# Linear attention with the states of two heads as blocks on a diagonal, and the levels of both pairs ahead of the chunks

## The chip, the cores and the metric

The kernel runs on one core of a Trainium2 chip. The metric is the time of one execution in microseconds (us) on the device. A core has five engines with an instruction stream each: PE (products), DVE, ACT and POOL (elementwise work) and SP, which issues the transfers here.

## The reference

One layer of a decoder for 2048 prompt tokens and 8 x 4 sample tokens, width 1024, in fp32. A mixer runs two kinds of heads beside each other, then there is cross-attention over 256 memory tokens, then a gated MLP with a convolution. The change lies in the gated linear attention (GLA) of the mixer: 4 heads, keys of 64 and values of 128 columns, evaluated in chunks:

```
q, k, v, r, a, u, sv = split_cols(xn @ w_in)
logg = log_sigmoid(a @ w_alpha + b_alpha) / 16
# per chunk, with b the running sum of logg in it:
scores = einsum('bihd,bjhd,bijhd->bijh', q, k, exp(b_i - b_j) where j <= i)
o = scores @ v + (q * exp(b)) @ S
S = exp(b_last) * S + (k * exp(b_last - b))^T @ v
# afterwards
o = rmsnorm(o, g_gla_out) * silu(r)
s_out = gelu(u) * z          # z: causal mixing of sv in chunks of 128
y = concat([o, s_out]) @ w_out
```

## The kernel before

The prompt goes through in four blocks s = 0 to 3 of 512 tokens; the 32 sample tokens ride along with block 1 in the mixer and with block 2 in the MLP. Names carry the block first: `v20` is tile 0 of v in block 2, `op213` is pair 1, chunk 3 in block 2.

A wide fp32 product is done as three products of split operands (hi by hi, lo by hi, hi by lo; lines L92 to L94), which accumulate in one of four PSUM banks of the pool accp. The projection of a block is a row of such steps: `t_ws` (sv), `a_wk`, `a_wq`, `t_wv` (v), `a_wu` (u), `t_wr` (r); then comes the output projection `a_wo`. A result is copied from its bank by DVE (v, r; L800) or goes through gelu on ACT (u, sv), and the next step's product that takes the bank waits for that. The split of a weight takes ACT (h_...) and DVE (l_..., L85).

The GLA goes two heads (a pair p) at a time, with 64 + 64 key columns on the 128 partitions. `sel` is a mask of 128 x 2 with a column for each head. Its steps for a pair:

- `diag`: the diagonal of the scores (pr on POOL, dgp on PE, dgs on DVE, P on ACT).
- seven `level` steps: level l gives the scores between the two halves of blocks of 2^(l+1) tokens. DVE subtracts (e), ACT takes exp, DVE makes kr (two instructions, one for each head), POOL multiplies e by k, PE makes s (four products), DVE copies s into P of both heads under a mask. `s206` is level 6 of pair 0 in block 2.
- `decay`: exp(b) on ACT; qz, which is q times exp(b) times sel, one tile for each head, on DVE; ebl (exp(b) at each chunk's end); kh, and its transpose ktp, which DVE copies to kt.
- four `chunk` steps (128 tokens): op on PE (for each head P times v, then qz times S, 128 columns each), which DVE copies to o; kv on PE, for each head a product of its 64 key columns on a half of the 128 x 64 positions; then DVE updates S, of 128 x 128, into the other of two buffers.

The sample's state has a step of its own (`smp`) in block 1. The tail: `onorm` (squares of o on ACT, L825, sums in oss; then rt on DVE, L298, and ors on POOL, L299), `silu` of r on ACT, `gate` (o times ors times r, DVE L1113), `back` (transposes otp, and the split ch20 to ch23). The SGU has zp on PE, z on DVE (L865), z times u on POOL (L875), and the split into ch24 to ch27 (ACT, L84) and cl24 to cl27 (POOL, L85); a_wo takes all eight.

The order in the program comes from `weave`: the projection's steps and w_out's are the main row, and a part (steps, first, last) is spread evenly over the main steps first to last. `gla_steps` returned its steps and its tail, and the call had the numbers:

```
(gla[:2], 5, 7), (gla[2:12], 8, 10), (gla[12:], 10, 13), (gtail, 16, 18)
```

`gla[:2]` are the gates and pair 0's running sums; `gla[2:12]` diag, pair 1's sums, seven levels and decay of pair 0; the rest four chunks of pair 0, then diag, levels, decay and chunks of pair 1. A scheduler then sets the order on each engine from the dependencies and its own estimate of durations; tiles come from rotating pools (49 wide ones in `up`), and every engine runs its stream in order.

## Time and profile before

| | us |
|---|---|
| median of 3 runs | 2885.29 |
| lowest, highest run | 2882.75, 2885.83 |
| the profiled execution, its own time | 2885.16 |
| its span, first to last instruction | 2883.4 |
| PE busy | 2847.6 |
| DVE busy | 1792.6 |
| ACT busy | 1055.3 |
| POOL busy | 667.6 |

The mean granted clock of PE is 0.998. A row of the timeline gives the start in us, the length in us, the engine, the line, the operation, out<-in, the shapes and the count of instructions that were put together; in brackets the idle time of the engine before it and what ended it. A fp32 product that isn't split appears as two records. A row of the waits names who waited for whom: us in total, times, longest.

From 1588 to 1725 us, the linear attention of block 2 with the work around it, PE is busy for 134.60 of 137.00 us, DVE for 104.66, ACT for 65.71 and POOL for 39.61.

### The profile page before, as it was taken

How to read it: one execution, taken by the hardware profiler on the slowest of the kernel's cores; microseconds unless marked ns; L12 is line 12 of the kernel's file. 1: busy time of each engine (PE TensorE's matmuls, PEld its weight loads, DVE VectorE, ACT ScalarE, POOL GpSimd, SP SyncE). 2: the span in 40 equal slices, each digit the busy share in tenths (PEclk: the TensorE clock that was granted, in tenths of full speed). 3: DMA queues.
4: the chain of work that ended last, by engine and by line, in shares of the span. 5: the costliest groups of instructions: out<-in, count | busy, mean ns of one | idle time of the engine just before them, and what ended most of it. 6: DMA issues, size and time to landing. Idle time of an engine off the chain costs nothing.

```text
span 2883.4 us, 47388 instructions
## 1 busy us (share of the span) xinstructions
PE 2847.6 (99%) x18148; PEld 2517.3 (87%) x18148; DVE 1792.6 (62%) x3101; ACT 1055.3 (37%) x1908; POOL 667.6 (23%) x700
## 2 busy tenths in 40 slices
PE   8999999999999999999999999999999999999998
PEld 8888988888888798888887889899999888899998
DVE  7568468777656645555556773566666675474555
ACT  5536344334364423222124453422223534331221
POOL 1213112111132311222222221222223132132221
PEclk9999999999999999999999999999999999999999
DMA  9646579999932245878995214577775323577775
GB/s 311 198 153 210 186 251 339 328 338 335 336 103 61 67 145 184 299 277 277 322 319 192 74 45 165 197 254 258 260 268 199 107 71 107 181 257 262 278 279 182
DMA packets 359626, 625.49 MB, mean 217 GB/s; under 512 B 26683, under 2 KB 227326, under 8 KB 359400
## 3 DMA queue, kind: packets, MB, share of 16 engines
q1 hardware_dynamic: 359400, 622.46, 63.7%
q8 instruction: 144, 2.36, 0.3%
q14 instruction: 82, 0.67, 0.1%
HBM read 497.04 MB, written 125.31 MB: 216 GB/s over the span
## 4 chain that ended last, share of the span: by engine, by line
PE 92%; DVE 4%; ACT 2%; issue 1%; POOL 1%; DMA 0%; DVEq 0%; SPq 0%; POOLq 0%; ACTq 0%
PE d L92 6%; PE d L94 6%; PE d L93 6%; PE sc L94 2%; PE sc L93 2%; PE sc L92 2%; PE a_wo L92 2%; PE a_wo L94 2%; PE a_wo L93 2%; PE a_wx L92 2%; PE a_wx L94 2%; PE a_wx L93 2%; PE a_wup L93 1%; PE a_wg L93 1%; PE a_wg L92 1%; PE a_wg L94 1%
## 5 line engine op out<-in xcount | busy, mean ns | idle before, releaser
L92 PE MATMUL d<-acth,whi_wd 128*128 128x512 f32 (+2 forms) x720 | 244.9, 340 | 4.9 <-DVE h L1546 4.9
L93 PE MATMUL d<-actl,whi_wd 128*128 128x512 f32 (+2 forms) x720 | 242.7, 337 | 0.0
L94 PE MATMUL d<-acth,wlo_wd 128*128 128x512 f32 (+2 forms) x720 | 242.6, 337 | 0.0
L1546 DVE TENSOR_TENSOR h<-d,h 128x512 f32<-128x512 f32 (+1 forms) x232 | 133.0, 581 | 150.0 <-PE d L94 149.7
L1485 POOL TENSOR_TENSOR c<-c,bc_f 128x512 f32<-128x512 f32 (+1 forms) x88 | 137.6, 1567 | 140.0 <-ACT c L1484 139.3
L92 PEld LDWEIGHTS d<-acth,whi_wd 128*128 128x128 f32 x720 | 135.5, 188 | 20.4 <-DVE h L1546 5.7
L94 PEld LDWEIGHTS d<-acth,wlo_wd 128*128 128x128 f32 x720 | 135.2, 188 | 15.8 <-issue 1.6
L93 PEld LDWEIGHTS d<-actl,whi_wd 128*128 128x128 f32 x720 | 135.4, 188 | 14.4 <-issue 1.2
L1475 ACT ACTIVATE c<-g,colsb 128x512 f32<-128x512 f32 x88 | 71.7, 815 | 206.1 <-DVE g L1444 154.3
L92 PE MATMUL sc<-whi_qk,woh 128*128 128x256 f32 x512 | 144.3, 283 | 0.0
L94 PE MATMUL sc<-whi_qk,wol 128*128 128x256 f32 x512 | 144.3, 282 | 0.0
L93 PE MATMUL sc<-wlo_qk,woh 128*128 128x256 f32 x512 | 143.9, 282 | 0.0
L1507 POOL TENSOR_TENSOR c<-r_q_wup,c 128x512 f32<-128x512 f32 (+1 forms) x33 | 58.7, 1779 | 341.7 <-DVE r_q_wup L279 221.5
L1472 POOL COPY carry<-g 128x2 f32<-128x2 f32 x88 | 30.8, 350 | 435.1 <-DVE g L1444 433.0
L984 POOL TENSOR_TENSOR e<-e,k 128x512 f32<-128x512 f32 (+1 forms) x48 | 69.2, 1441 | 238.6 <-DVE kr L980 168.4
L92 PE MATMUL a_wo<-ch,h_wo 128*128 128x512 f32 (+1 forms) x320 | 113.3, 358 | 5.1 <-ACT ch L84 4.0
L94 PE MATMUL a_wo<-ch,l_wo 128*128 128x512 f32 (+1 forms) x320 | 113.2, 354 | 0.0
L93 PE MATMUL a_wo<-cl,h_wo 128*128 128x512 f32 (+1 forms) x320 | 112.9, 353 | 0.0
L1476 DVE SCALAR_TENSOR_TENSOR c<-g,colsb,c 128x512 f32<-128x512 f32 x88 | 86.0, 977 | 30.7 <-ACT c L1475 30.1
L92 PE MATMUL a_wx<-pTh,whi_wx 128*128 128x512 f32 x256 | 101.2, 395 | 0.0
L94 PE MATMUL a_wx<-pTh,wlo_wx 128*128 128x512 f32 x256 | 100.4, 392 | 0.0
L93 PE MATMUL a_wx<-pTl,whi_wx 128*128 128x512 f32 x256 | 100.3, 392 | 0.0
(3354 smaller groups left out, 9526.2 us busy)
## 6 DMA issues: line engine op xcount, KB each, us to landing
whi_wd<-wd SPq DMA_DIRECT2D x66, 512.0 KB
wlo_wd<-wd SPq DMA_DIRECT2D x66, 512.0 KB
r_wo<-in_w_out_dram SPq DMA_DIRECT2D x32, 512.0 KB
whi_qk<-qkd SPq DMA_DIRECT2D x32, 512.0 KB
wlo_qk<-qkd SPq DMA_DIRECT2D x32, 512.0 KB
wlo_wx<-vod SPq DMA_DIRECT2D x32, 512.0 KB
whi_wx<-vod SPq DMA_DIRECT2D x32, 512.0 KB
r_wg<-in_w_gate_dram SPq DMA_DIRECT2D x22, 512.0 KB
```

The costliest lines, as they stand in the source:

```text
L92: pe.matmul(ps, wh, xh, start=first, stop=False)
L93: pe.matmul(ps, wh, xl, start=False, stop=False)
L94: pe.matmul(ps, wl, xh, start=False, stop=last)
L984: pool.tensor_tensor(kl[:, :Tl], e[:, :Tl], B.k[p][:, :Tl], ALU.mult)
L1472: pool.tensor_copy(carry[:, f, :], g[:, SB:SB + 2])
L1475: act.activation(c[:, :SB], g[:, 2:SB + 2], AF.Identity, bias=cb, scale=w2)
L1476: dve.scalar_tensor_tensor(c[:, :SB], g[:, 1:SB + 1], w1, c[:, :SB], ALU.mult, ALU.add)
L1485: pool.tensor_tensor(c[:, :T], c[:, :T], B.fbc[:, :T], ALU.mult)
L1507: (dve, pool)[i].tensor_tensor(c[:, :T], q[i], c[:, :T], ALU.mult)
L1546: dve.tensor_tensor(B.h[m + mm][:, cs], ps[:, :cw], B.h[m + mm][:, cs], ALU.add)
```

## The change

- S of a pair is a tile of 128 x 256 with the two heads' states of 64 x 128 as blocks on its diagonal and zeros elsewhere. Two such tiles for each pair are set to zero at the start (POOL) and used in turn.
- qz is one tile for each pair, without sel.
- `chunk`: op is first one product of qz with S, 256 columns, and then two of P with v, 128 columns each; kv is one product of 128 x 256, of which the blocks on the diagonal are used; S is updated by two DVE instructions of 64 x 128.
- The squares of o are taken in `chunk` (and `smp`) after pair 1 of that chunk.
- `smp` masks qz for each head on DVE first (qm).
- The order: outside block 1, levels of pair 0 over main steps 7 to 9, levels of pair 1 over 9 to 12, and then all eight chunks over 12 to 14. In block 1 the parts stand as before.
- The final state leaves in four transfers in place of two; `up` has 48 wide tiles in place of 49.

```diff
-NU, NT, NRAW, NW = 49, 6, 5, 5
+NU, NT, NRAW, NW = 48, 6, 5, 5
...
-        t = cp.tile([128, 128], F32, tag=f"S{p}", name=f"Sz{p}", bufs=2)
-        pool.memset(t, 0.0)
-        state[p] = t
+        state[p] = [const([128, 256], f"S{p}{i}") for i in range(2)]
+        for t in state[p]:
+            pool.memset(t, 0.0)
...
-            for hh in range(2):
-                z = U(f"qz{s}{p}{hh}")
-                dve.scalar_tensor_tensor(z[:, :T], B.q[p][:, :T], sel[:, hh:hh + 1], e0[:, :T], ALU.mult, ALU.mult)
-                B.qz[2 * p + hh] = z
+            z = U(f"qz{s}{p}")
+            dve.tensor_tensor(z[:, :T], B.q[p][:, :T], e0[:, :T], ALU.mult)
+            B.qz[p] = z
...
-            S = state[p]
+            S, Sn = state[p]
             cs = slice(c * 128, (c + 1) * 128)
+            pe.matmul(ps[:, :256], B.qz[p][:, cs], S, start=True, stop=False)
             for hh in range(2):
                 h = 2 * p + hh
-                os_ = slice(hh * 128, (hh + 1) * 128)
-                pe.matmul(ps[:, os_], B.P[h][:, cs], B.v[c][:, h * 128:(h + 1) * 128], start=True, stop=False)
-                pe.matmul(ps[:, os_], B.qz[h][:, cs], S, start=False, stop=True)
+                pe.matmul(ps[:, hh * 128:(hh + 1) * 128], B.P[h][:, cs], B.v[c][:, h * 128:(h + 1) * 128],
+                          start=False, stop=hh == 1)
             dve.tensor_copy(B.o[c][:, p * 256:(p + 1) * 256], ps[:, :256])
             kv = mps(f"kv{s}{p}{c}")
+            pe.matmul(kv[:, :256], B.kt[p][:, cs], B.v[c][:, p * 256:(p + 1) * 256], start=True, stop=True)
             for hh in range(2):
-                h = 2 * p + hh
-                pe.matmul(kv[hh * 64:(hh + 1) * 64, :128],
-                          B.kt[p][:, c * 128 + hh * 64:c * 128 + (hh + 1) * 64],
-                          B.v[c][:, h * 128:(h + 1) * 128], start=True, stop=True)
-            Sn = cp.tile([128, 128], F32, tag=f"S{p}", name=f"S{s}{p}{c}", bufs=2)
-            dve.scalar_tensor_tensor(Sn, S, B.eb[p][:, c:c + 1], kv[:, :128], ALU.mult, ALU.add)
-            state[p] = Sn
-            if s == NSB - 1 and c == 3:
-                nc.sync.dma_start(o_state_gla[0, 0, 2 * p:2 * p + 2].rearrange("hh d v -> (hh d) v"), Sn)
+                rows, os_ = slice(hh * 64, (hh + 1) * 64), slice(hh * 128, (hh + 1) * 128)
+                dve.scalar_tensor_tensor(Sn[rows, os_], S[rows, os_], B.eb[p][rows, c:c + 1], kv[rows, os_],
+                                         ALU.mult, ALU.add)
+                if s == NSB - 1 and c == 3:
+                    nc.sync.dma_start(o_state_gla[0, 0, 2 * p + hh], Sn[rows, os_])
+            state[p] = Sn, S
+            if p == 1:
+                norm_of(B.o[c], B.oss, c, 128)
...
-                pool.tensor_tensor(qm3, blkbc, B.qz[h][:, SB:TM].unsqueeze(1).broadcast_to([128, 8, NS]), ALU.mult)
+                dve.tensor_scalar(qm[:, 256:288], B.qz[p][:, SB:TM], sel[:, hh:hh + 1], None, ALU.mult)
+                pool.tensor_tensor(qm3, blkbc, qm[:, 256:288].unsqueeze(1).broadcast_to([128, 8, NS]), ALU.mult)
...
-            for c in range(nt):
-                norm_of(B.o[c], B.oss, c, 128 if c < 4 else NS)
             rstd_of20(B.ors, B.oss, sample, 1.0 / 128)
...
+        if sample:
+            parts = [(head, 5, 7), (pairs[0], 8, 10), (ends[0] + pairs[1] + ends[1], 10, 13), (tail, 16, 18)]
+        else:
+            parts = [(head, 5, 7), (pairs[0], 7, 9), (pairs[1], 9, 12), (ends[0] + ends[1], 12, 14), (tail, 16, 18)]
```

How the order moves, at three places of block 2.

PE in the kernel before, from the first chunk of pair 1 on (S113 and S210 are the states after the chunks 113 and 210):

```order
L1052 MATMUL op210_16874<-v20_16404,P210_16536 128x128
L1053 MATMUL op210_16874<-S113_9584,qz210_16811 128x128
L1052 MATMUL op210_16874<-v20_16404,P211_16541 128x128
L1053 MATMUL op210_16874<-S113_9584,qz211_16813 128x128
L1058 MATMUL kv210_16880<-v20_16404,kt21_16826 64x128 x2
L1052 MATMUL op211_16885<-v21_16405,P210_16536 128x128
L1058 MATMUL kv211_16891<-v21_16405,kt21_16826 64x128 x2
L1052 MATMUL op212_16896<-v22_16406,P210_16536 128x128
L1053 MATMUL op211_16885<-S210_16883,qz210_16811 128x128
```

PE in the changed kernel at the same place (S10 and S11 are the two tiles for the state of pair 1):

```order
L1050 MATMUL op210_16832<-S10_245,qz21_16729 128x256
L1053 MATMUL op210_16832<-v20_16466,P210_16416 128x128
L1053 MATMUL op210_16832<-v20_16466,P211_16421 128x128
L1057 MATMUL kv210_16837<-v20_16466,kt21_16742 128x256
L1050 MATMUL op211_16845<-S11_246,qz21_16729 128x256
L1053 MATMUL op211_16845<-v21_16467,P210_16416 128x128
L1053 MATMUL op211_16845<-v21_16467,P211_16421 128x128
L1057 MATMUL kv211_16850<-v21_16467,kt21_16742 128x256
L862 MATMUL zp22_16888<-wsT_688,sv20_15897 128x128
```

The products of P with v and the next kv stood ahead of the products with S210; now op211 begins with the product with S11, which DVE makes from kv210, the row just ahead.

DVE in the kernel before, from the masks of level 3 of pair 0 on (e205 and kr205 belong to level 5, kh20 to decay):

```order
L995 COPY_PREDICATED P200_16272<-mask3_129,s203_16370 128x32x8
L995 COPY_PREDICATED P201_16277<-mask3_129,s203_16370 128x32x8
L800 COPY v20_16404<-t_wv20_16205 128x512
L980 SCALAR_TENSOR_TENSOR kr205_16434<-e205_16430,sel_153,q20_16142 128x256 x2
L969 TENSOR_TENSOR e206_16445<-b20_16197 128x4x64
L970 TENSOR_TENSOR e206_16445<-b20_16197 128x4x64
L995 COPY_PREDICATED P200_16272<-mask4_135,s204_16385 128x16x16
L995 COPY_PREDICATED P201_16277<-mask4_135,s204_16385 128x16x16
L800 COPY v21_16405<-t_wv21_16212 128x512
L800 COPY v22_16406<-t_wv22_16219 128x512
L980 SCALAR_TENSOR_TENSOR kr206_16449<-e206_16445,sel_153,q20_16142 128x256 x2
L1020 TENSOR_TENSOR kh20_16468<-b20_16197 128x512
```

DVE in the changed kernel, from the masks of level 6 of pair 0 on (e211 and e212 are levels 1 and 2 of pair 1, dgs21 its diagonal):

```order
L996 COPY_PREDICATED P200_16210<-mask6_147,s206_16383 128x4x64
L996 COPY_PREDICATED P201_16215<-mask6_147,s206_16383 128x4x64
L970 TENSOR_TENSOR e211_16439<-b21_16225 128x128x2
L971 TENSOR_TENSOR e211_16439<-b21_16225 128x128x2
L1032 COPY kt20_16405<-ktp20_16400 128x512
L85 TENSOR_TENSOR l_wr20_16457<-r_wr20_16454,h_wr20_16456 128x1024
L945 COPY dgs21_16408<-dgp21_16407 128x8
L981 SCALAR_TENSOR_TENSOR kr211_16443<-e211_16439,sel_153,q21_16137 128x256 x2
L970 TENSOR_TENSOR e212_16492<-b21_16225 128x64x4
L971 TENSOR_TENSOR e212_16492<-b21_16225 128x64x4
L800 COPY v20_16466<-t_wv20_16173 128x512
L800 COPY v21_16467<-t_wv21_16180 128x512
```

The copy of v20 stood between the masks of level 3 and kr of level 5 of pair 0; now it stands behind pair 0's last masks, kt20, the split l_wr20 and two levels' worth of pair 1.

POOL in the kernel before, the end of the SGU, and ors:

```order
L875 TENSOR_TENSOR z22_16953<-z22_16953,u22_16723 128x512
L875 TENSOR_TENSOR z23_16995<-z23_16995,u23_16750 128x512
L299 TENSOR_TENSOR ors2_17041<-rt_17058,neghalf_88 128x16
L85 TENSOR_TENSOR cl26_16957<-z22_16953,ch26_16956 128x512
L85 TENSOR_TENSOR cl27_16999<-z23_16995,ch27_16998 128x512
```

POOL in the changed kernel, the same five instructions:

```order
L875 TENSOR_TENSOR z22_16893<-z22_16893,u22_16671 128x512
L85 TENSOR_TENSOR cl26_16897<-z22_16893,ch26_16896 128x512
L299 TENSOR_TENSOR ors2_16749<-rt_17006,neghalf_88 128x16
L875 TENSOR_TENSOR z23_16961<-z23_16961,u23_16698 128x512
L85 TENSOR_TENSOR cl27_16965<-z23_16961,ch27_16964 128x512
```

z23 times u went ahead of ors and now goes behind it; cl26 went behind ors and now goes ahead. On PE the first products of a_wo took ch24 to ch26 and left cl26, ch27 and cl27 for later; now they take ch24 to ch27 with their cl in a row.

More of the change, by code (lines that the diff above doesn't have):

```diff
@@ L1045, in chunk @@
                 B.o = [U(f"o{s}{i}") for i in range(nt)]
+                B.oss, B.ors = narrow(f"oss{s}", 20), narrow(f"ors{s}", 20)
             ps = mps(f"op{s}{p}{c}")
-            S = state[p]
+            S, Sn = state[p]
             cs = slice(c * 128, (c + 1) * 128)
+            pe.matmul(ps[:, :256], B.qz[p][:, cs], S, start=True, stop=False)
             for hh in range(2):
                 h = 2 * p + hh
-                os_ = slice(hh * 128, (hh + 1) * 128)
-                pe.matmul(ps[:, os_], B.P[h][:, cs], B.v[c][:, h * 128:(h + 1) * 128], start=True, stop=False)
-                pe.matmul(ps[:, os_], B.qz[h][:, cs], S, start=False, stop=True)
+                pe.matmul(ps[:, hh * 128:(hh + 1) * 128], B.P[h][:, cs], B.v[c][:, h * 128:(h + 1) * 128],
+                          start=False, stop=hh == 1)
             dve.tensor_copy(B.o[c][:, p * 256:(p + 1) * 256], ps[:, :256])
             kv = mps(f"kv{s}{p}{c}")
+            pe.matmul(kv[:, :256], B.kt[p][:, cs], B.v[c][:, p * 256:(p + 1) * 256], start=True, stop=True)
             for hh in range(2):
-                h = 2 * p + hh
-                pe.matmul(kv[hh * 64:(hh + 1) * 64, :128],
-                          B.kt[p][:, c * 128 + hh * 64:c * 128 + (hh + 1) * 64],
-                          B.v[c][:, h * 128:(h + 1) * 128], start=True, stop=True)
-            Sn = cp.tile([128, 128], F32, tag=f"S{p}", name=f"S{s}{p}{c}", bufs=2)
-            dve.scalar_tensor_tensor(Sn, S, B.eb[p][:, c:c + 1], kv[:, :128], ALU.mult, ALU.add)
-            state[p] = Sn
-            if s == NSB - 1 and c == 3:
-                nc.sync.dma_start(o_state_gla[0, 0, 2 * p:2 * p + 2].rearrange("hh d v -> (hh d) v"), Sn)
+                rows, os_ = slice(hh * 64, (hh + 1) * 64), slice(hh * 128, (hh + 1) * 128)
[6 more added lines that the diff above has]
+                norm_of(B.o[c], B.oss, c, 128)
         sgd = state_gla[0].rearrange("b (p hh) d v -> (hh d) b p v", hh=2)
@@ L1083, in smp @@
             dve.tensor_copy(B.o[4][:NS, p * 256:(p + 1) * 256], ps[:NS, :256])
+            if p == 1:
+                norm_of(B.o[4], B.oss, 4, NS)
             for i in range(2):
@@ L1099, in onorm @@
         def onorm():
-            B.oss, B.ors = narrow(f"oss{s}", 20), narrow(f"ors{s}", 20)
-            for c in range(nt):
-                norm_of(B.o[c], B.oss, c, 128 if c < 4 else NS)
             rstd_of20(B.ors, B.oss, sample, 1.0 / 128)
@@ L1127, in back @@
             B.cat[h] = (hi, lo)
-        out = [gates, lambda: cums(0)]
+        head, pairs, ends = [gates, lambda: cums(0)], [], []
         for p in range(2):
-            out.append(lambda p=p: diag(p))
-            if p == 0:
-                out.append(lambda: cums(1))
-            out += [lambda p=p, l=l: level(p, l) for l in range(7)]
-            out.append(lambda p=p: decay(p))
-            out += [lambda p=p, c=c: chunk(p, c) for c in range(4)]
-            if sample:
-                out.append(lambda p=p: smp(p))
+            pairs.append([lambda p=p: diag(p)] + ([lambda: cums(1)] if p == 0 else [])
+                         + [lambda p=p, l=l: level(p, l) for l in range(7)] + [lambda p=p: decay(p)])
+            ends.append([lambda p=p, c=c: chunk(p, c) for c in range(4)] + ([lambda p=p: smp(p)] if sample else []))
         tail = [onorm] + [lambda c=c: silu(c) for c in range(nt)] + [lambda c=c: gate(c) for c in range(nt)]
         tail += [lambda h=h: back(h) for h in range(4)]
-        return [Step(f) for f in out], [Step(f) for f in tail]
+        if sample:
+            parts = [(head, 5, 7), (pairs[0], 8, 10), (ends[0] + pairs[1] + ends[1], 10, 13), (tail, 16, 18)]
+        else:
+            parts = [(head, 5, 7), (pairs[0], 7, 9), (pairs[1], 9, 12), (ends[0] + ends[1], 12, 14), (tail, 16, 18)]
+        return [([Step(f) for f in x], i, j) for x, i, j in parts]
     def out_proj_steps(B, unit, src, g, name, sample, first, finished, keep=None, seven=False,
@@ L1624, in hymba_step_kernel @@
         proj = proj_steps(B)
-        gla, gtail = gla_steps(B)
+        gla = gla_steps(B)
         sgu_st = sgu_steps(B)
@@ L1636, in hymba_step_kernel @@
         folds = [(qk_steps, 0, 10), (vo_steps, 11, 19)] if s == 0 else []
-        steps += weave(proj + w1, *folds, (after, 0, 5), (sgu_st[:1], 6, 6), (sgu_st[1:nst], 11, 11), (sgu_st[nst:], 12, 15), (gla[:2], 5, 7), (gla[2:12], 8, 10), (gla[12:], 10, 13), (gtail, 16, 18))
+        steps += weave(proj + w1, *folds, (after, 0, 5), (sgu_st[:1], 6, 6), (sgu_st[1:nst], 11, 11), (sgu_st[nst:], 12, 15), *gla)
         scales, sc, turns = attention_steps(B)
```

## The prediction

> **What bounds the kernel.** I read the page first (busy shares, the chain that ended last), then the waits of PE, then the timeline of PE, DVE, ACT and POOL around the linear attention. The first two rows below are the page's, the others the waits of PE.

> ```profile
> PE 2847.6 (99%) x18148; PEld 2517.3 (87%) x18148; DVE 1792.6 (62%) x3101; ACT 1055.3 (37%) x1908; POOL 667.6 (23%) x700
> ...
> PE 92%; DVE 4%; ACT 2%; issue 1%; POOL 1%; DMA 0%; DVEq 0%; SPq 0%; POOLq 0%; ACTq 0%
> ...
> PE a_wo L92 <- ACT ch L84: 4.0, 2, 2.0
> ...
> PE s L991 <- POOL e L984: 1.9, 4, 1.1
> ...
> PE op L1052 <- DVE o L1054: 0.6, 1, 0.6
> ```

> PE is busy for 99% of the span and is 92% of the chain. A change can win in two ways only: less time on PE, or fewer of the few microseconds in which PE waits. It loses when PE comes to a product whose operand is late. The profiled execution took 2885.16 us, the median of the three runs is 2885.29; the sum is made against 2885.2. A measurement of this kernel can tell about 0.2% (5.8 us) from no change.

> **The products (PE).** The timeline of PE in block 0, where products of a chunk stand among those of the projection, then a product of 256 columns (lgp, whose 8 records are 4 products):

> ```profile
> 201.53 0.39 PE L92 MATMUL a_wu<-xh,h_wu 128*128 128x512 f32 x1
> 201.76 0.40 PE L93 MATMUL a_wu<-xl,h_wu 128*128 128x512 f32 x1
> 202.09 0.44 PE L1058 MATMUL kv<-v,kt 128*64 128x128 f32 x4
> 202.46 0.49 PE L1052 MATMUL op<-v,P 128*128 128x128 f32 x2
> 202.88 0.44 PE L1058 MATMUL kv<-v,kt 128*64 128x128 f32 x4
> 203.24 0.50 PE L94 MATMUL a_wu<-xh,l_wu 128*128 128x512 f32 x1
> 203.58 0.40 PE L92 MATMUL a_wu<-xh,h_wu 128*128 128x512 f32 x1
> ...
> 127.91 1.99 PE L911 MATMUL lgp<-wal,aT 33*128 33x256 f32 x8
> ```

> A wide product starts 0.23 after the one ahead (201.53, 201.76), so without the chunk the next would start at 201.99. It starts at 203.24, and the one behind it 0.34 later instead of 0.23: the insertion cost 1.25 + 0.11 = 1.36. An op of 128 columns is 0.22 (below, 1700.93 to 1701.15), so two kv pairs cost 1.14, one 0.57, though its four records are only 0.44 long. A chunk before is 4 x 0.22 + 0.57 = 1.45. A record of 256 columns takes (1.99 - 0.39) / 7 = 0.23, a product two of them, 0.46. A chunk after is 0.46 (q times S) + 0.44 (two P times v) + 0.46 (kv) = 1.36. That saves 0.09, times 32 chunks: **-2.9**. Ends: +1.3 if the old kv pair is worth only its 0.44, -6.4 if each pair has the 0.11 for itself too.

> The two tiles of a kv pair run at once (four records in 0.44). [...]

> **From chunk to chunk.** Before, P times v of a chunk and the next kv went ahead of the product with S, so PE had work while DVE made the new S. Now an op begins with the product with S. By the built order nine chunks follow directly on the kv of the chunk that makes their S, same pair, with nothing between (two in each of blocks 0, 2 and 3, three in block 1). The chain there, in rows of PE, DVE and POOL of block 2:

> ```profile
> 1700.93 0.39 PE L1053 MATMUL op<-S,qz 128*128 128x128 f32 x2
> 1701.15 1.95 PE L862 MATMUL zp<-wsT,sv 128*128 128x128 f32 x16
> ...
> 1701.36 0.42 DVE L1054 COPY o<-op 128x256 f32<-128x256 f32 x1 [0.51 <-PE op L1053]
> ...
> 1699.05 0.35 DVE L1062 SCALAR_TENSOR_TENSOR S<-S,ebl,kv 128x128 f32<-128x128 f32 x1
> ...
> 1687.31 1.29 POOL L984 TENSOR_TENSOR e<-e,k 128x512 f32<-128x512 f32 x1 [2.44 <-DVE kr L980]
> ...
> 1688.65 1.16 PE L991 MATMUL s<-kr,e 128*128 128x128 f32 x8 [0.29 <-POOL e L984]
> ```

> PE could go on 0.22 after the start of an op's last product, whose result is there at 0.39: 0.17 late. DVE begins 0.04 later (1701.32 to 1701.36). S is now two updates of 64 partitions and 128 elements; one of 128 x 128 took 0.35, and a pair of independent DVE instructions starts 0.08 closer than their length (1630.40 and 1630.73, next rows): 0.35 + 0.27 = 0.62. Ends 0.35 (at once) and 0.70 (in full). PE starts 0.05 after its operand (1688.60 to 1688.65). Sum 0.17 + 0.04 + 0.62 + 0.05 = 0.88, nine times: **+7.9** (5.5 to 8.6).

> **Levels of both pairs ahead, and the copies of v.** A projection's result is copied out of its PSUM bank by DVE, and the first a_wu product takes the bank of t_wv20 over. Before, v20 was copied between two levels, at 1629.01. Now pair 0's levels end a step earlier, pair 1's begin there, and the four copies of v stand on DVE behind P206, e211, kt20, l_wr20, dgs21, kr211 and e212. On PE only four wide products, ktp20, dgp21 and s210 stand between s206 and a_wu. DVE's prices (block 2; kt from later in it):

> ```profile
> 1627.21 1.21 DVE L85 TENSOR_TENSOR l_wu<-r_wu,h_wu 128x1024 fp32r<-128x1024 f32 x1
> 1628.35 0.75 DVE L995 COPY_PREDICATED P<-mask,s 128x256 f32<-128x256 uint8 x2
> 1629.01 0.68 DVE L800 COPY v<-t_wv 128x512 f32<-128x512 f32 x1
> 1629.61 0.87 DVE L980 SCALAR_TENSOR_TENSOR kr<-e,sel,q 128x256 f32<-128x256 f32 x2
> 1630.40 0.41 DVE L969 TENSOR_TENSOR e<-b 128x256 f32<-128x256 f32 x1
> 1630.73 0.41 DVE L970 TENSOR_TENSOR e<-b 128x256 f32<-128x256 f32 x1
> 1631.07 0.77 DVE L995 COPY_PREDICATED P<-mask,s 128x256 f32<-128x256 uint8 x2
> ...
> 1694.46 0.69 DVE L1032 COPY kt<-ktp 128x512 f32<-128x512 f32 x1 [0.34 <-PE ktp L1030]
> ```

> By the distance of starts: P 0.66, e 0.67, kt 0.60, the split l_wr as l_wu 1.14, dgs 0.1 (my guess for 8 columns), kr 0.79, e 0.67, v 0.68, PE's start 0.05: 5.36 after s206. PE's cover is 4 x 0.23 + 4 x 0.22 + 0.2 (four tiny dgp, a guess) + 4 x 0.22 = 2.9. PE waits 2.4 in block 2, and in block 3, whose order is the same. In block 0 no split is in the way but the wide products are not either: 0.66 + 0.60 + 0.79 + 0.67 + 0.1 + 0.68 + 0.05 = 3.55 against 2.0, so 1.55. Block 1 keeps its order. Together **+6.35**. Ends: 0 if DVE is far ahead; 9.4 if DVE is a microsecond late at the start in each. Queued behind v20 on DVE are v21 to v23 and the masks of s210; a_wu's first group is 24 products (5.5 us), which covers them.

> **The tail of blocks 2 and 3.** Rows of PE, DVE, POOL and ACT at the end of block 2:

> ```profile
> 1705.11 0.47 PE L92 MATMUL a_wo<-ch,h_wo 128*128 128x512 f32 x1 [2.01 <-ACT ch L84]
> ...
> 1705.89 0.63 PE L92 MATMUL a_wo<-ch,h_wo 128*128 128x512 f32 x1
> ...
> 1709.30 0.39 PE L93 MATMUL a_wo<-cl,h_wo 128*128 128x512 f32 x1
> ...
> 1702.25 1.64 DVE L865 SCALAR_TENSOR_TENSOR z<-zp,colsb,bsb 128x512 f32<-128x512 f32 x2 [0.47 <-PE zp L862]
> 1703.86 0.51 DVE L298 TENSOR_SCALAR rt<-oss 128x16 f32<-128x16 f32 x1
> 1704.29 2.47 DVE L800 COPY r<-t_wr 128x512 f32<-128x512 f32 x4
> ...
> 1703.08 2.50 POOL L875 TENSOR_TENSOR z<-z,u 128x512 f32<-128x512 f32 x2 [2.54 <-DVE z L865]
> 1705.54 2.90 POOL L299 TENSOR_TENSOR ors<-rt,neghalf 128x16 f32<-128x16 f32 x1
> 1708.41 2.59 POOL L85 TENSOR_TENSOR cl<-z,ch 128x512 fp32r<-128x512 f32 x2
> ...
> 1703.42 0.31 ACT L825 ACTIVATE junk<-o 128x128 bf16<-128x128 f32 x1
> 1703.64 0.19 ACT L825 ACTIVATION_READ_ACCUMULATOR junk<-o 128x1 f32 x1
> 1704.38 0.63 ACT L84 ACTIVATE ch<-z 128x512 fp32r<-128x512 f32 x1 [0.55 <-POOL z L875]
> ```

> PE waits 2.01 for a_wo, which the waits put down to ch; in the program its bank waits for the copy of r20, which stands behind rt, which waits for the last square (1703.83, rt at 1703.86). After: o23 is copied 0.46 after op213's end; its four squares take 4 x 0.42 with ch26 (0.63) among them, 2.3; rt 0.43, z23 0.8, r20 0.65, start 0.05: 4.7 after op213's end. PE's cover behind op213 is kv213 0.46 and zp23 0.88, less the 0.17: 1.2 (zp22 has moved ahead of op212). A wait of 3.5 against 2.0; but squares of earlier chunks have more time now, and z23 may meet no queue, so I take +1.2 of the 1.5, twice: **+2.4** (ends -4.0, the wait gone, and +4).

> Then a_wo meets ch27 and cl27. Before, their products came 27 or more wide products later; now a_wo's first group takes ch24 to ch27 in a row, and POOL does ors (2.9) ahead of z23 times u. With t0 the start of rt, ors ends at t0 + 3.4, z23 times u (1.25) at 4.65, ch27 at 5.35, cl27 (1.3) at 6.65. a_wo starts about t0 + 1.95 and has nine products (2.07) up to ch27: it waits 1.35, does one, and waits 1.1 for cl27. 2.45 in each block: **+4.9** (0 to 5.5).

> **What goes.** The wait for o (0.6) and three of the four waits for e (1.9 less the longest, 1.1: 0.8) stand where the change moves the levels: **-1.4** (0 to -1.9). After the wait at 1705.11 eight products run 0.43 apart instead of 0.23 until 1709.30, as if at half speed, 1.6 lost; I leave that as it is, 0.

> **What costs nothing.** One qz in place of two frees DVE about 0.7 a pair, beside PE. Squares: the same 16 on ACT. Two memsets more on POOL at the start, before its first work. Four transfers of the final state instead of two on SP's queue in block 3, 500 us before the end. Four small DVE products for qm in block 1, once. One buffer fewer, but qz needs two fewer. The moved levels issue no DMA.

> Sum: -2.9 + 7.9 + 6.35 + 2.4 + 4.9 - 1.4 = +17.2; 2885.2 + 17.2 = **2902** us.

> **Rivals.** "Hidden": DVE and ACT run ahead, v20 and the tail cost nothing new. For it: before, v20 was copied the moment its product ended. 2885.2 - 2.9 + 7.9 - 1.4 = 2889, within 0.2%. "Squares early", the faster one: rt is released at the last square, 2.05 after o23 was copied (1701.78 to 1703.83). If squares by chunk take that backlog away and DVE copies r20 before zp23 ends, the 2.0 goes in both blocks and the 1.6 with it, cl27 arrives in time, and with products at -6.4 and chunk waits at 5.5 the time is 2885.2 - 6.4 + 5.5 - 1.4 - 5.6 = 2877. It decides where the last square ends less than 0.1 after op213's cover; ch26 between the squares speaks against it. "Half speed": each new wait of 2 to 3 us is followed by a stretch as at 1705.89. Three more: 2902 + 4.8 = 2907. [...]

> **Chances.** Forecast 0.58, hidden 0.15, squares early 0.09, half speed 0.12, pairs 0.06. Slower by over 0.2%: 0.58 + 0.12 + 0.06 = 0.76; within 0.15; faster 0.09. The forecast's own range is 2893 to 2910, from its terms' ends taken a few at a time. Leaving out squares early and pairs and most of what lies past hidden gives 2886 to 2913.

> **What would show it.** Right: PE waits of about 0.9 ahead of op for S at nine places, one of 2 to 3 us ahead of a_wu for v in blocks 2 and 3, two waits inside a_wo's first group for ch and cl, products of op and kv about 3 us cheaper in all. Wrong: a_wu starting right behind s210, or a_wo's waits no longer than 2 us in all. If DVE's S updates overlap other work, the chunk term falls to half.

## The result, and the profile after

The changed kernel takes 2913.86 us (median; 2910.09 to 2915.89), the kernel before 2885.29 beside it: ratio 1.0101, 95% interval 1.009 to 1.0111. It is 28.6 us slower. Forecast were 2902 us, 17 slower; the direction was right, the size too small, and the time lies outside the range.

The page of the changed kernel, busy times and the chain that ended last:

```profile
PE 2854.5 (98%) x18020; PEld 2528.6 (87%) x18020; DVE 1787.3 (61%) x3129; ACT 1054.0 (36%) x1906; POOL 673.0 (23%) x702
...
PE 91%; DVE 4%; issue 2%; ACT 1%; DMA 1%; POOL 0%; DVEq 0%; SPq 0%; POOLq 0%; ACTq 0%
```

PE was busy for 7 us more, although it has fewer products, and the span is 29.7 us longer (2913.1). The waits of PE:

```profile
PE op L1050 <- DVE S L1060: 13.6, 9, 2.1
PE a_wu L92 <- DVE v L800: 6.9, 2, 3.4
PE a_wo L92 <- DVE r L800: 4.6, 3, 1.8
...
PE s L992 <- DVE kr L981: 2.5, 1, 2.5
...
PE a_wo L92 <- ACT ch L84: 2.2, 2, 1.1
...
PE a_wo L93 <- POOL cl L85: 1.7, 2, 0.9
...
PE ktp L1030 <- POOL kh L1027: 1.2, 2, 0.6
...
PE dgp L944 <- POOL pr L941: 1.0, 1, 1.0
```

Nine waits of op for S, two of a_wu for v, the pair for ch and cl in blocks 2 and 3: all three kinds that were forecast are there. The waits for e (1.9) and for o (0.6) of before are gone. PE at the end of block 2, first the chunks of pair 1, then a_wo:

```profile
1711.33 0.60 PE L1057 MATMUL kv<-v,kt 128*128 128x256 f32 x2
1711.76 0.60 PE L1050 MATMUL op<-S,qz 128*128 128x256 f32 x2
1712.19 0.61 PE L1053 MATMUL op<-v,P 128*128 128x128 f32 x4
1712.64 0.60 PE L1057 MATMUL kv<-v,kt 128*128 128x256 f32 x2
1715.26 0.87 PE L1050 MATMUL op<-S,qz 128*128 128x256 f32 x2 [2.02 <-DVE S L1060]
...
1721.57 0.67 PE L1050 MATMUL op<-S,qz 128*128 128x256 f32 x2 [0.91 <-DVE S L1060]
...
1725.81 0.47 PE L92 MATMUL a_wo<-ch,h_wo 128*128 128x512 f32 x1 [1.80 <-DVE r L800]
...
1729.23 0.50 PE L92 MATMUL a_wo<-ch,h_wo 128*128 128x512 f32 x1 [1.10 <-ACT ch L84]
1730.57 0.50 PE L93 MATMUL a_wo<-cl,h_wo 128*128 128x512 f32 x1 [0.84 <-POOL cl L85]
```

From kv to kv (1711.33 to 1712.64) a chunk takes 1.31 where nothing waits, 0.14 less than the 1.45 of before. At 1721.57 stands the plain wait for S; at 1715.26 one of 2.02. DVE of the same stretch tells them apart:

```profile
1711.74 1.23 DVE L85 TENSOR_TENSOR l_wo<-r_wo,h_wo 128x1024 fp32r<-128x1024 f32 x1 [1.95 <-ACT h_wo L84]
1712.89 0.70 DVE L1060 SCALAR_TENSOR_TENSOR S<-S,ebl,kv 64x128 f32<-64x128 f32 x2
1713.60 0.76 DVE L1055 COPY o<-op 128x256 f32<-128x256 f32 x2
1714.39 0.72 DVE L1060 SCALAR_TENSOR_TENSOR S<-S,ebl,kv 64x128 f32<-64x128 f32 x2
```

kv210 was done at 1713.2, but DVE had a weight's split, the other pair's S and two copies of o to do first, and made S at 1715.1.

One thing more is in the granted clock: in the kernel before PE had half its clock in four stretches (from 989.07, 1705.87, 1856.06 and 2880.06 us), in the changed kernel in nine, of 3.4, 6.8 or 8.3 us. Six of the nine begin in or just behind a wait that the change brought (186.43, 271.76, 920.29, 1650.75, 1715.60 and 2340.24); at the places of the other three (998.80, 2234.43 and the end) PE waits in the kernel before too. Two rows of the changed kernel, each of 8 us that begin in the last part of a wait for v (the column ahead of the last two is the clock):

```profile
1650.00:1658.00 8.00, 6.29 (x16) 4.95 (x17) 7.02 (x15) 3.23 (x10) 3.36 (x3) 0.57 0.20 67
2339.00:2347.00 8.00, 5.08 (x12) 4.03 (x13) 7.22 (x17) 3.60 (x10) 2.98 (x2) 0.58 0.22 66
```

For an account I took from each trace the distance from one product's start to the next, less the product's own time at full speed. Excesses above 0.3 us are waits; smaller ones inside a stretch at half speed are its loss; the rest is what the products themselves cost.

| kernel | median us | ratio to before, interval | waits of PE | lost at half speed |
|---|---|---|---|---|
| before | 2885.29 | | 31.4 | 4.6 |
| after | 2913.86 | 1.009 to 1.0111 | 57.4 | 15.6 |
| e1 order back | 2920.01 | 1.0098 to 1.013 | 59.3 | 16.4 |
| e2 P with v first | 2909.93 | 1.0066 to 1.0096 | 47.4 | 18.0 |
| e3 both | 2885.57 | 0.999 to 1.0009 | 31.8 | 8.6 |
| e4 order only | 2910.22 | 1.0071 to 1.0103 | 49.0 | 12.0 |
| e5 filler for v | 2910.69 | 1.0073 to 1.0101 | 49.7 | 11.3 |
| e6 levels later | 2908.70 | 1.0064 to 1.0092 | 54.9 | 3.1 |
| e7 squares back | 2886.38 | 0.9995 to 1.0013 | 31.3 | 10.2 |
| e8 squares by pair | 2890.71 | 1.0007 to 1.0025 | 33.9 | 13.8 |
| e9 filler for v and S | 2908.15 | 1.0063 to 1.0094 | 38.8 | 8.4 |
| e10 filler in the tail | 2884.19 | 0.9987 to 1.0005 | 27.9 | 5.9 |
| e11 two repairs | 2894.89 | 1.0019 to 1.0044 | 39.3 | 9.2 |
| e12 filler, block 1 too | 2886.76 | 0.9994 to 1.0012 | 24.6 | 7.3 |

The account is of one execution of each kernel, and where it parts waits from products depends on its limit of 0.3. From before to after the waits grew by 26.1, the loss at half speed by 10.9, and the span by 29.7: that leaves 7.3 which the products saved. In the same way the kernels with the merged products and without filler come to between 2.7 (e6) and 7.3, and e4, whose products are those of before, to 0.4.

### The profile page after: what moved, and what is told of

The parts are those of the page before. It is cut to its first block, busy times and chain, and to the rows that moved or that the text cites. A ratio compares the mean times of both kernels' runs of the same rounds, so it can differ in the third digit from the quotient of the medians.

```text
span 2913.1 us, 47191 instructions
## 1 busy us (share of the span) xinstructions
PE 2854.5 (98%) x18020; PEld 2528.6 (87%) x18020; DVE 1787.3 (61%) x3129; ACT 1054.0 (36%) x1906; POOL 673.0 (23%) x702
## 4 chain that ended last, share of the span: by engine, by line
PE 91%; DVE 4%; issue 2%; ACT 1%; DMA 1%; POOL 0%; DVEq 0%; SPq 0%; POOLq 0%; ACTq 0%
PE d L92 6%; PE d L94 6%; PE d L93 6%; PE sc L94 2%; PE sc L93 2%; PE sc L92 2%; PE a_wo L93 2%; PE a_wo L92 2%; PE a_wo L94 2%; PE a_wx L94 2%; PE a_wx L93 2%; PE a_wx L92 2%; PE a_wup L93 1%; PE a_wg L93 1%; PE a_wg L94 1%
## 5 line engine op out<-in xcount | busy, mean ns | idle before, releaser
L92 PE MATMUL d<-acth,whi_wd 128*128 128x512 f32 (+2 forms) x720 | 245.9, 342 | 3.6 <-DVE h L1546 3.6
L94 PE MATMUL d<-acth,wlo_wd 128*128 128x512 f32 (+2 forms) x720 | 243.4, 338 | 0.0
L93 PE MATMUL d<-actl,whi_wd 128*128 128x512 f32 (+2 forms) x720 | 243.3, 338 | 0.0
L92 PEld LDWEIGHTS d<-acth,whi_wd 128*128 128x128 f32 x720 | 136.2, 189 | 18.7 <-DVE h L1546 4.3
L94 PEld LDWEIGHTS d<-acth,wlo_wd 128*128 128x128 f32 x720 | 136.2, 189 | 15.5 <-issue 1.2
L93 PEld LDWEIGHTS d<-actl,whi_wd 128*128 128x128 f32 x720 | 136.3, 189 | 14.2 <-issue 1.2
L94 PE MATMUL sc<-whi_qk,wol 128*128 128x256 f32 x512 | 144.2, 282 | 0.0
L92 PE MATMUL sc<-whi_qk,woh 128*128 128x256 f32 x512 | 144.2, 283 | 0.0
L93 PE MATMUL sc<-wlo_qk,woh 128*128 128x256 f32 x512 | 143.5, 282 | 0.0
L92 PE MATMUL a_wo<-ch,h_wo 128*128 128x512 f32 (+1 forms) x320 | 113.9, 357 | 6.8 <-DVE r L800 4.6
L93 PE MATMUL a_wo<-cl,h_wo 128*128 128x512 f32 (+1 forms) x320 | 113.6, 355 | 1.7 <-POOL cl L85 1.7
L94 PE MATMUL a_wo<-ch,l_wo 128*128 128x512 f32 (+1 forms) x320 | 112.9, 353 | 0.0
L92 PE MATMUL a_wx<-pTh,whi_wx 128*128 128x512 f32 x256 | 101.4, 396 | 0.0
L93 PE MATMUL a_wx<-pTl,whi_wx 128*128 128x512 f32 x256 | 100.8, 394 | 0.0
L94 PE MATMUL a_wx<-pTh,wlo_wx 128*128 128x512 f32 x256 | 100.7, 393 | 0.0
```

Of the source, the lines that this page charges most:

```text
L92: pe.matmul(ps, wh, xh, start=first, stop=False)
L93: pe.matmul(ps, wh, xl, start=False, stop=False)
L94: pe.matmul(ps, wl, xh, start=False, stop=last)
```

## The experiments

**e1: the order of before.**

```diff
-            parts = [(head, 5, 7), (pairs[0], 7, 9), (pairs[1], 9, 12), (ends[0] + ends[1], 12, 14), (tail, 16, 18)]
+            parts = [(head, 5, 7), (pairs[0], 8, 10), (ends[0] + pairs[1] + ends[1], 10, 13), (tail, 16, 18)]
```

> Edit: the changed kernel with the order of before in every block (levels and chunks of a pair together). Theory 1 (the loss has two sources of new waits, an op that begins with the product with S, and the levels moved ahead, each with half speed behind its waits; the products themselves are cheaper): the waits of a_wu for v and of a_wo for ch and cl go, but 13 chunks now follow directly on the kv that makes their S, about 1.2 us each, 15 in all; with products about 6 cheaper and some 4 of half speed: 2898 us (2892 to 2904). Theory 2 (the order alone costs): 2880, below the kernel before. Theory 3 (the merged products are dearer): 2905 or more.

2920.01 us, 6 more than the changed kernel and 22 more than expected. Two waits of PE in e1:

```profile
PE op L1050 <- DVE S L1060: 16.8, 13, 2.1
PE t_wr L92 <- ACT u L801: 6.0, 2, 3.0
```

The waits for S were counted right (15 expected). Two waits of 3 us for the gelu of u came with this order, and 16.4 were lost at half speed instead of some 8 (4.6 and 4 more). The order alone is not the cause: theory 2 is out. The time is in the range of theory 3, but not by its mechanism: by the account the products save 4.7 here (waits 27.9 and half speed 11.8 more than before, span 35.0 longer).

**e2: P with v first.**

```diff
-            pe.matmul(ps[:, :256], B.qz[p][:, cs], S, start=True, stop=False)
             for hh in range(2):
                 h = 2 * p + hh
                 pe.matmul(ps[:, hh * 128:(hh + 1) * 128], B.P[h][:, cs], B.v[c][:, h * 128:(h + 1) * 128],
-                          start=False, stop=hh == 1)
+                          start=hh == 0, stop=False)
+            pe.matmul(ps[:, :256], B.qz[p][:, cs], S, start=False, stop=True)
```

> Edit: the changed kernel with the two products of P with v first in an op and the product with S last, as in the kernel before. Theory 1: the nine waits of op for S (13.6 us) go nearly all and about 4 us of half speed with them: 2896 us (2891 to 2901); the waits of a_wu for v stay at 3.4 us each. Theory 2 (order alone): no change from 2914. Theory 3 (dearer products): no change from 2914 either.

2909.93: only 4 us won, 18 expected. Two waits of PE, and a row of DVE in block 2:

```profile
PE a_wo L92 <- DVE r L800: 10.4, 4, 4.5
...
PE op L1054 <- DVE S L1060: 2.6, 2, 1.6
...
1716.38 0.18 DVE L298 TENSOR_SCALAR rt<-oss 128x16 f32<-128x16 f32 x1 [2.84 <-ACT junk L825]
```

The waits for S fell from 13.6 to 2.6 as expected, but the last product with S now came behind zp23, o23 was copied later, the squares ended later, and a_wo waited 4.5 us for r in blocks 2 and 3. Its waits for ch and cl (3.9 in the changed kernel) are gone in turn, so that a_wo waits 10.4 in place of 8.5. All waits together fell by 10.0 (57.4 to 47.4) and the span by 5.3 (2913.1 to 2907.8): half speed took 2.4 more, 18.0, and the other 2.3 are in what the account leaves to the products.

**e3: both back.** The edits of e1 and e2 together.

> Edit: both, the order of before and P with v first; what stays of the change are the merged products of 256 columns, the halved updates of S, one qz and squares by chunk. Theory 1: 2880 us (2876 to 2884), faster than the kernel before by what the products save. Theory 3 (dearer products): 2890 or more.

2885.57: as the kernel before, not faster (2880 was expected). The account says that the products save 3.9 here (span 0.5 longer, waits 0.4 and half speed 4.0 more). A wait of PE in e3:

```profile
PE a_wo L92 <- ACT ch L84: 7.0, 3, 3.3
```

a_wo waits 3.3 in blocks 2 and 3 (2.0 before): in block 2 PE is through with zp23 2.05 us earlier than before (at 1701.05, not 1703.10), but the copy of r20, behind ACT's squares, begins only 0.82 earlier (1703.47, not 1704.29). What the products give, the tail and its half speed take.

**e4: the order alone**, on the kernel before: its `gla_steps` with the lists `head`, `pairs`, `ends` and the `parts` of the change.

> Edit: the kernel before with nothing but the new order (levels of both pairs ahead of the chunks). Theory 1: the waits of a_wu for v (about 3 us in blocks 2 and 3), the waits in block 0 (3.5) and some half speed behind them: 2899 us (2892 to 2905). Theory that the order is harmless and the loss lies in op and its wait for S: 2885.

2910.22, 25 us slower, and above the 2892 to 2905 that were expected. Waits of PE in e4:

```profile
PE a_wu L92 <- DVE v L800: 7.7, 2, 4.1
PE a_wo L92 <- DVE r L800: 7.4, 4, 3.0
PE s L991 <- DVE kr L980: 4.6, 3, 3.8
...
PE dgp L943 <- POOL pr L940: 3.2, 3, 1.5
```

The waits for v are those of the changed kernel. The diagonal and level 0 of pair 1, now between t_wv and a_wu, wait for pr and kr in blocks 0, 2 and 3, 3.8 us at the longest in block 0. So the order alone is worth nearly the whole loss, and an op that begins with S (e1) is as well; they do not add. My reading is that either puts PE ahead of DVE, and the next thing that PE needs is late.

**e5: filler in the wait for v**, in the changed kernel.

```diff
             for c in range(4):
                 pe.matmul(ps3[:, :, c * 64:(c + 1) * 64], kl[:, c * 128:(c + 1) * 128],
                           kr3[:, :, c * 64:(c + 1) * 64], start=True, stop=True)
+            if s >= 2 and p == 1 and l == 0:
+                fl = mps(f"fill{s}")
+                for i in range(14):
+                    pe.matmul(fl, B.xs[0][0][:, :128], B.xs[0][0][:, :SB], start=True, stop=True)
```

> Edit: the changed kernel with 14 products of 128x512 that nobody reads (0.23 us each, 3.2 in all) between s210 and the first a_wu, in blocks 2 and 3. Theory (a wait of some 3 us makes the products behind it run at half speed, and this is a cost of its own): PE stays busy through the wait for v, the wait shrinks from 3.4 to about 0.2, and the seven us at half speed behind it run at full speed, some 2.7 us gained in each of the two blocks: 2908.5 us. Rival (half speed comes at its own times, whatever PE did before): 2914, or more by what the filler exceeds the wait.

2910.69, 3.2 less than the changed kernel with 28 products more. PE in block 2, and the same two stretches of 8 us as above:

```profile
1648.14 3.44 PE L997 MATMUL fill<-xh 128*128 128x512 f32 x14
1651.82 0.51 PE L92 MATMUL a_wu<-xh,h_wu 128*128 128x512 f32 x1 [0.24 <-DVE v L800]
...
1650.00:1658.00 8.00, 7.76 (x38) 6.19 (x38) 7.62 (x18) 4.48 (x11) 3.32 (x2) 1.00 0.23 69
2339.00:2347.00 8.00, 7.76 (x38) 6.42 (x38) 7.62 (x16) 4.05 (x8) 3.41 (x3) 1.00 0.16 54
```

a_wu starts at the same time (1651.82 against 1651.70), so DVE's lateness is untouched; the clock is 1.00 instead of 0.57, and 38 products (7 of them filler) run in the first stretch instead of 16. Half speed behind a wait is a cost of its own. Product by product: the first a_wu of block 2 starts 0.12 later in e5, and the a_wu product that the changed kernel starts at 1659.09 starts at 1656.52, so 2.7 were gained on the way, as the theory says. In block 3 it is 2.4 (2341.92 and 2339.38, then 2350.12 and 2345.22). The spans differ by 4.9 (2913.1 and 2908.2), the medians by 3.2, with intervals that overlap.

**e6: the levels of pair 1 a step later**, in the changed kernel.

```diff
-... (pairs[0], 7, 9), (pairs[1], 9, 12), ...
+... (pairs[0], 7, 9), (pairs[1], 10, 12), ...
```

> Edit: the changed kernel with the levels of pair 1 over main steps 10 to 12 instead of 9 to 12, so that the four copies of v stand on DVE ahead of l_wr20, kr211 and e212 (1.14 + 0.1 + 0.79 + 0.67 = 2.7 less to wait for). Theory (the copies of v are late because of what the moved levels put ahead of them): the wait of a_wu for v falls from 3.4 to below 1 us in blocks 2 and 3, and with half speed the time falls by 8 to 10: 2905 us. Rival (DVE is late as a whole): the wait only moves to the next product that needs DVE, 2912 or more.

2908.70. PE in block 2, and its waits:

```profile
1643.47 0.50 PE L92 MATMUL a_wu<-xh,h_wu 128*128 128x512 f32 x1 [0.77 <-DVE v L800]
...
PE op L1050 <- DVE S L1060: 14.7, 11, 2.0
...
PE ktp L1030 <- POOL kh L1027: 3.9, 5, 1.1
```

The wait for v fell from 3.44 to 0.77, by the 2.7 that had stood ahead on DVE. But the sum of the waits fell by 2.5 only: ktp waits 2.7 more for kh, op 1.1 more. Both theories had a part of it: the time is between 2905 and 2912. The profiled execution was the fastest of its four (2904.48) and had the least half speed of all, 3.1.

**e7: squares in onorm again**, on e3 (norm_of is taken out of `chunk` and `smp` and put back in `onorm`).

> Edit: order of before and P with v first, as in e3, and the squares of o in onorm again, as before; the merged products, halved updates of S and the single qz stay. Theory (squares by chunk cost nothing or little, the products save about 4 us, and the tail waits for ACT's 16 squares in either case): 2885 us, as e3. Rival (squares by chunk put ch behind them and make a_wo wait 3.3 instead of 2): 2881.

2886.38, as e3: squares by chunk neither cost nor bring anything measurable.

**e8: squares of a pair behind its chunk**, on e3.

```diff
-            if p == 1:
-                norm_of(B.o[c], B.oss, c, 128)
+            for h in (2 * p, 2 * p + 1):
+                act.activation(junk[:, :128], B.o[c][:, h * 128:(h + 1) * 128], AF.Square,
+                               accum_out=B.oss[:, c * 4 + h:c * 4 + h + 1])
```

> Edit: as e3, but the squares of a pair's two heads right after that pair's chunk, so that 8 and not 16 of them (0.43 us each) stand behind the last chunks. Theory (rt waits for the last square, and a_wo for r20 behind rt): the last square comes about 3 us earlier and the wait of a_wo, 3.3 in blocks 2 and 3, falls below 2, with less half speed behind it: 2880 us. Rival (DVE's z and the copies of r hold a_wo, not the squares): 2885, as e3.

2890.71, slower than e3. Waits of PE, and DVE in block 2:

```profile
PE a_wo L92 <- DVE r L800: 6.4, 3, 2.7
...
PE a_wo L93 <- POOL cl L85: 2.0, 2, 1.2
...
1701.52 1.19 DVE L298 TENSOR_SCALAR rt<-oss 128x16 f32<-128x16 f32 x1 [0.18 <-ACT junk L1066]
1702.63 0.74 DVE L865 SCALAR_TENSOR_TENSOR z<-zp,colsb,bsb 128x512 f32<-128x512 f32 x1
1703.29 2.47 DVE L800 COPY r<-t_wr 128x512 f32<-128x512 f32 x4
```

rt did come a microsecond earlier (1701.52; e3: 1702.59), but now z23 stood between it and r20, so a_wo gained only 0.6, and ors ahead of z23 on POOL brought back the wait for cl. In all, the waits are 2.1 longer than in e3, and half speed took 5.2 more. So the squares are not all that holds a_wo, as the rival says; that the kernel gets slower neither side expected.

**e9: filler for S too.** As e5, and behind the kv of the nine chunks:

```diff
+            if (s, p, c) in ((0, 1, 0), (0, 1, 2), (1, 0, 2), (1, 1, 1), (1, 1, 2), (2, 1, 0), (2, 1, 2), (3, 1, 0), (3, 1, 2)):
+                fl = mps(f"fc{s}{p}{c}")
+                for i in range(4):
+                    pe.matmul(fl, B.xs[0][0][:, :128], B.xs[0][0][:, :SB], start=True, stop=True)
```

> Edit: as e5, and four such unread products (0.92 us) behind the kv of each of the nine chunks that are followed by the chunk that needs their S. Theory (half speed is a cost of its own, some 11 us more in the changed kernel than before, and follows PE's idle time): the waits of op for S shrink from 13.6 to about 6, the time in them stays the same since filler takes their place, and the half speed behind them goes: 2906 us, with half the stretch at half speed of e5. Rival (filler only adds work): 2911 or more.

2908.15, 2.5 less than e5 with 8.3 us of filler more; 2906 and 2911 were expected, and its interval overlaps that of e5. The wait of PE for S:

```profile
PE op L1054 <- DVE S L1068: 3.4, 5, 1.1
```

In blocks 2 and 3 the filler itself waits 0.51 for S. 8.4 are lost at half speed in place of 11.3 (e5) and 15.6 (after): less, not half.

**e10: filler in the tail**, on e3: 12 such products behind zp23 in blocks 2 and 3.

> Edit: as e3 (order of before, P with v first), and 12 unread products of 128x512 (2.8 us) behind zp23 in blocks 2 and 3, where a_wo waits 3.3 us. Theory: the wait falls to about 0.5, the stretch at half speed behind it (3.4 to 6.8 us of it, 1.6 to 3.3 lost) goes: 2881 us, faster than before and after. Rival (no half speed to be gained): 2886 or more.

2884.19, where 2881 and 2886 were expected: the fastest median here, though its interval (0.9987 to 1.0005) doesn't set it apart from the kernel before. PE in block 2:

```profile
1702.36 2.98 PE L884 MATMUL fill<-xh 128*128 128x512 f32 x12
1705.92 0.47 PE L92 MATMUL a_wo<-ch,h_wo 128*128 128x512 f32 x1 [0.58 <-ACT ch L84]
```

The half speed behind a_wo's start in blocks 2 and 3 is gone from the trace; e3 had 6.8 and 3.4 us of it there.

**e11: two repairs**, the edits of e2 and e6 in the changed kernel.

> Edit: the changed kernel with both repairs in its own order: P with v first, and the levels of pair 1 a step later (e2 and e6 together). Theory: the waits of op for S (13.6) and of a_wu for v (6.9) are gone, what stays are the waits of the tail, where the last product with S now stands behind zp23 and a_wo waits for r20 3 to 4 us in blocks 2 and 3, and block 0's: 2899 us. Rival (the two repairs hide the same loss): 2908, as the better of the two alone.

2894.89, better than either alone (2909.93, 2908.70) and than expected. The largest of the waits that stay is in the tail:

```profile
PE a_wo L92 <- DVE r L800: 8.4, 4, 3.5
```

**e12: filler in block 1 too**, on e10: six products ahead of the product with S of op113, five ahead of a_wo.

> Edit: as e10, and unread products in block 1 too: six (1.4 us) ahead of the product with S of op113, which waits 1.6, and five (1.15 us) ahead of a_wo, which waits 1.0 to 1.3. Theory: the 3.4 to 10 us at half speed that stand in block 1 at 977 to 994 us in nearly every execution go, 1.6 to 3 us gained: 2881.5 us, faster than the kernel before by 0.1%. Rival (block 1's half speed comes from its many small products, not from the waits): 2884, as e10.

2886.76, where 2881.5 and 2884 were expected, and 2.6 more than e10: nothing gained. A wait of PE in e12, then the row of block 1 from 982 us:

```profile
PE fc L1064 <- DVE S L1071: 1.7, 1, 1.7
...
982.00:996.50 14.50, 13.91 (x95) 11.76 (x94) 9.09 (x25) 5.49 (x11) 8.46 (x6) 0.76 0.26 74
```

The six products (fc) didn't do what they were meant for: PE waits for S ahead of them, and they come on top of that wait. The five did take the place of a_wo's wait, but the half speed begins before it, at 989.44. PE is busy for 13.91 of 14.50 us, and the clock is 0.76 all the same. Earlier in block 1 of e12 it falls to a half with no wait at all, from 842.67 on:

```profile
839.68:841.39 1.71, 1.71 (x9) 1.39 (x8) 1.71 (x11) 1.41 (x2) 0.67 (x1) 1.00 0.00 0
841.39:843.09 1.70, 1.70 (x9) 0.96 (x9) 1.70 (x8) 1.67 (x3) 0.00 (x0) 0.88 0.04 10
843.09:844.80 1.71, 1.71 (x9) 1.71 (x9) 1.71 (x6) 1.69 (x4) 0.00 (x0) 0.50 0.00 0
```

PE is busy throughout these rows. In the kernel before, the ten records of lgp with 33 rows each run at this place, from 839.75 to 842.29, and the clock stays at 1.00 in the same three rows; in e12 it falls to 0.50. Many products of the sample have 32 columns or 32 rows. Whether such products make the clock fall was not tried; by these rows it falls without a wait too.

## Why the prediction was wrong

The waits that were forecast came, all three kinds of them; the sum was 11 us short. Two terms carry the miss: half speed, which I put at nothing, and the waits behind DVE, which I priced as if DVE stood ready. Term by term, measured in the rows above:

- **Half speed** was set to 0, with a rival at 2907 for three more stretches. It is 10.9 us in the profiled execution. This is the step that failed most. I had the row of a wait of 2.0 with half speed behind it (1705.89) and added some twenty microseconds of new waits without the stretches behind them. The rival had the mechanism, but three new stretches, where six began at new waits. e5 shows the price of one kind directly: nearly the same start of a_wu, and 2.7 and 2.4 us behind it in blocks 2 and 3.
- **From chunk to chunk**: 7.9 forecast, 13.6 measured. The number of places was right (nine). The plain wait is 0.91, at three of the nine. That looks like the 0.88 of the forecast, but the forecast counted from where PE could have gone on, 0.17 ahead of where the row's idle time begins; counted so, it is 1.08, with the pair of updates at 0.72, near the end "in full" and not at 0.62, and PE 0.16 behind them, not 0.05 (the updates end at 1721.41, op starts at 1721.57). The other six waits are 1.36 to 2.06 long. DVE had work of other steps queued ahead there, as the rows from 1711.74 on show for one of them: I priced the chain as if DVE stood ready.
- **The copies of v**: 2.4 in each of blocks 2 and 3, measured 3.44 and the like (6.9 in all). From P206 to a_wu DVE took 5.32 (1646.38 to 1651.70), as forecast (5.36). But kr210, which I had left out, stood ahead of P206 and waited 0.57 for its exp, so that P206 began 2.1 behind the end of s206 (1644.24; the two rows of DVE stand below this list). PE came later too, by 0.65 at ktp20 among other things, so its wait grew by 1.0 only. The 0.2 for four dgp was a guess that no run shows: by the distance of starts dgp21 takes 0.81 (1646.32 to 1647.13); dgs21, guessed at 0.1, takes 0.08 (1649.44 to 1649.52). In block 0 the wait (1.55 forecast) came as 2.5 for kr and 1.0 for pr, at s010 and dgp01. 6.35 forecast, 10.4 with these, 11.6 with ktp's 1.2 (0.4 before).
- **The tail**: ch and cl 4.9 forecast, 3.9 measured, place by place (1.35 and 1.1 against 1.10 and 0.84). The growth of a_wo's first wait (2.4) did not come: 4.6 now, 5.0 before (4.0 and 1.0). The squares of earlier chunks had in fact been done by then.
- **Products**: -2.9 forecast; 1.31 a chunk instead of 1.45 makes -4.5, the account gives -3.9 in e3, where nothing else differs much, and -7.3 in the changed kernel. No run shows dearer products, "pairs" among the chances: the merged ones are cheaper by these figures, although the two tiles of a kv pair had run at once (four records in 0.44).
- **What goes**: -1.4 forecast, 2.5 gone.

```profile
1645.20 1.25 DVE L981 SCALAR_TENSOR_TENSOR kr<-e,sel,q 128x256 f32<-128x256 f32 x2 [0.57 <-ACT e L975]
1646.38 0.76 DVE L996 COPY_PREDICATED P<-mask,s 128x256 f32<-128x256 uint8 x2
```

The sum of measured terms, 13.6 + 11.6 + 3.9 - 0.4 - 2.5 - 4.5 + 10.9 = 32.6, is above the 29.7 of the span. The waits among these terms come to 26.2, as in the account (26.1), so the gap lies in the products: 4.5 by the rows of one chunk, 7.3 by the account. Which is nearer is open; the idle time of a row is not the whole delay of the product behind it, as the 0.91 and 1.08 above show.

"Squares early" is out: e7 and e8 show no gain. "Hidden" is out too: a_wu waits for v, and a_wo for ch and cl.

What the experiments add to the forecast is how the parts hang together. The order alone costs 25 us (e4), and an op that begins with S costs 34 more than its counterpart in the order of before (e1 against e3), but only 4 in the new order (e2). The waits read as if they shared a cause: PE is put ahead of DVE, and where one wait is taken away, PE comes sooner to the next one (e2's to the tail, e6's to ktp and op). Only with both taken back does the loss go (e3), and with P with v first and the new order a step later two thirds of it (e11).

## What to carry to other kernels

A product that needs the result of the instruction just ahead should be last in its group, so that independent products stand between (34 us here in the order of before, 4 in the new one); and the copies that free a projection's bank should be written ahead of the steps that are woven in (e6: the wait for v fell from 3.44 to 0.77). On an engine that is busy for 99% of the span, price a new wait with what DVE has queued ahead of its releaser (1.36 to 2.06 here at six of nine places, 0.91 at the other three), and add half speed behind it (10.9 here in all). Before counting on the removal of one wait, look for what is late next.
